# Scaling x by its norm once, before the split, instead of scaling the projections on POOL

## The chip, the cores and the metric

One Trainium2 chip, one core of it. The metric is the device time of one execution in microseconds, as the median of several runs; lower is better. A profile of one execution gives the rows that are quoted below. The engines go by short names: PE is TensorE (matmuls; PEld is its weight load), DVE is VectorE, ACT is ScalarE, POOL is GpSimd, and SP is the engine whose queue issues most DMAs.

## The reference

The kernel computes one layer of a hybrid decoder for 256 tokens of width 1024 in float32, with a final norm:

```python
h = rmsnorm(x, ln_w)                        # x * rsqrt(mean(x*x) + eps) * ln_w
proj = einsum('bsd,de->bse', h, w_in)       # 1024 -> 9216 columns
rq, rk, rv, rg, mq, mk, mv, mg, gr, gm = split(proj)
ret = head_groupnorm(retention(rq, rk, rv)) * silu(rg) @ w_ret_o
mo  = moba_attention(mq, mk, mv) * silu(mg) @ w_moba_o
y   = sigmoid(gr) * ret + sigmoid(gm) * mo
out = rmsnorm(x + y @ w_out, final_norm_w)
```

The norm of x is one number per token. So it can be applied to x ahead of the projection, or to the projection behind it: both give the same product.

## The kernel before, in words

All matrix products run as 24 groups of 512 weight columns, group 0 to group 23. Groups 0 and 1 give the retention's v, groups 2 and 3 its q and k, groups 4 to 9 q, k and v of the other attention (MoBA), groups 10 to 17 the gates, groups 18 to 21 the two branch outputs, groups 22 and 23 the last projection. K is 1024, cut into 8 tiles of 128. The weights of a group come in four chunks of two K tiles (`load`, L77, 512 KB each; the tile `raw` has 6 buffers).

Every operand is split into a high and a low part of 12-bit significands, so that three fast products replace one slow one. For weights that is `split` (L95): ACT copies to `wh` (L108), DVE subtracts to get `wl` (L109); both have 8 buffers, which is two groups. For x it is `split_x` (L149): ACT writes `xh`, DVE `xl` (L152), both with the norm weight of the feature as a scalar, K tile by K tile as x arrives. The norm of the token is not in them.

A group is either N (tokens on the partitions, `proj_n`, L186, three 512-column products per K tile and token tile at L195 to L197) or T (features on the partitions, `proj_t`, L200, per K tile and feature tile a 512-column product at L210 and a 256-column one at L211; four feature tiles per group). The results lie in 4 PSUM banks (`pm`), one per token tile or feature tile.

The norm is computed from a second copy of x: `x_stats` (L168, one number per token and partition, `rs`) and `x_stats_t` (L177), in which PE turns `rs` into a row over all partitions (L180), DVE copies it to `rsb` (L182) and ACT makes `rsq`, the same with the attention's factor (L183). N results are scaled by `rs` as they leave PSUM, at no instruction of their own. T results leave PSUM in `evac_t` (L365): ACT copies one half (L370), DVE adds the other (L371), and POOL multiplies by `rsb` or `rsq` (L372). For q and k there follows `split_to` (L237): ACT copies the high part (L238), POOL subtracts (L239).

The program is written as units, two per group: unit u = 2 * group + half. Ahead of a unit stand the splits of two chunks of the next group, the loads of the group after that, and attention pieces. Each engine executes its own queue in order. The order within the queues is laid out ahead of time by a planner, which lets an engine take the earliest instruction of the program that its estimates call ready; so products of several feature tiles are interleaved when the operands of one are late. On the chip nothing is reordered any more: an instruction that waits holds up all that stand behind it on its engine.

`ret_scores` (L293) makes the masked scores of a retention head: DVE multiplies (L299), ACT and DVE split (L302, L303), and `ret_pv` (L306) is the product with v (L314 to L316).

Of the kernel before, what the change touches and what calls it, by code (L numbers as in the profile page):

```python
"""Hybrid decoder layer (RMSNorm, retention branch, MoBA branch, gated merge, residual, final RMSNorm)
for 256 tokens of width 1024 on one core.

Layouts: a tensor is "N" with tokens on the partitions and "T" with features on the partitions.
Each projection is either N (activations stationary, weights moving, 512 columns) or T (weights
stationary, activations moving, 256 tokens), so that the consumer finds the layout that it needs.

Products with at least 256 moving columns run in float32r (12-bit significands, one pass each): every
operand a is split exactly into a = ah + al with ah = round12(a), al = a - ah, and ah*bh + ah*bl + al*bh are
accumulated in float32. Attention products with 128 moving columns are plain float32 matmuls.  # L10

With 256 tokens the MoBA branch has a single block of 256, so no query has a past block: the top-k
selection is empty for any input, and each query attends causally to its own block.
"""
# [15 lines left out]
P = 128  # L30
# [18 lines left out]
def hybrid_kernel(ctx: ExitStack, tc, xT, x, w_in, gn_w, w_ret_o, w_moba_o, w_out, fn_w, decay, out):  # L49
# [41 lines left out]
    def cut(g, k):  # L91
        """Column ranges in which K tile k of group g is handled."""
        return (slice(0, S), slice(S, GW)) if (g, k) == (0, 0) else (slice(0, GW),)
# [24 lines left out]
    # K tile 0 of group 0 comes in two column ranges: its banks are started by products of zeros.  # L118
# [18 lines left out]
    # rel[q, k] = k - q for the causal pairs, MASKED for the others; query tile 0 with keys 0..127,  # L137
    # query tile 1 with keys 0..255.
# [6 lines left out]

    xs = ac.tile([P, KT, 2, S], F32R, name="xs", tag="xs")
    xh, xl = xs[:, :, 0], xs[:, :, 1]

    def split_x(k):  # L149
        xk = xt[:, KT + k * S:KT + (k + 1) * S]  # L150
        nc.scalar.activation(xh[:, k], xk, AF.Copy, scale=lnw[:, k:k + 1])
        nc.vector.scalar_tensor_tensor(xl[:, k], xk, lnw[:, k:k + 1], xh[:, k].bitcast(F32),  # L152
                                       op0=ALU.mult, op1=ALU.subtract)

    def rsqrt(y, a, tmp):
        """y = a ** -0.5 (a is kept): square root, exact reciprocal, one Newton step."""
        nc.scalar.activation(tmp, a, AF.Sqrt)
        nc.vector.reciprocal(y, tmp)
        nc.vector.tensor_mul(tmp, y, y)
        nc.vector.tensor_mul(tmp, tmp, a)  # L160
        nc.vector.tensor_scalar(tmp, tmp, -0.5, 1.5, op0=ALU.mult, op1=ALU.add)
        nc.vector.tensor_mul(y, y, tmp)
# [3 lines left out]
    rsq = cst.tile([P, S], F32, name="rsq")  # L166

    def x_stats():  # L168
        """1 / rms per token: per partition for N, along the free axis for T."""
        ss = cst.tile([P, NT], F32, name="ss")  # L170
        tmp = cst.tile([P, NT], F32, name="sst")
        for t in range(NT):
            nc.scalar.activation(reto[:, t], xn[:, t], AF.Square, accum_out=ss[:, t:t + 1])
        nc.vector.tensor_scalar(ss, ss, 1.0 / D, EPS, op0=ALU.mult, op1=ALU.add)
        rsqrt(rs, ss, tmp)

    def x_stats_t():  # L177
        ps = pa.tile([P, 512], F32, name="ps_s", tag="s")
        for t in range(NT):
            nc.tensor.matmul(ps[:, t * P:(t + 1) * P], rs[:, t:t + 1].to_broadcast([P, P]), ident,  # L180
                             start=True, stop=True)
        nc.vector.tensor_copy(rsb, ps[:, :S])  # L182
        nc.scalar.activation(rsq, ps[:, :S], AF.Copy, scale=1.0 / math.sqrt(P))  # L183

# [1 line left out]
    def proj_n(g, ah, al, t, c0=0, n=GW, ps=None):  # L186
        """[128 tokens of tile t, n columns of the group from c0], added to ps if that is given."""
# [4 lines left out]
        for k in range(KT):  # L192
            for cs in cut(g, k) if g == 0 else (slice(0, n),):
                h, l = (w[g, k // 2][:, k % 2, c0 + cs.start:c0 + cs.stop] for w in (wh, wl))
                nc.tensor.matmul(ps[:, cs], ah[:, k, sl], h, start=not begun and k == 0, stop=False)  # L195
                nc.tensor.matmul(ps[:, cs], ah[:, k, sl], l, start=False, stop=False)  # L196
                nc.tensor.matmul(ps[:, cs], al[:, k, sl], h, start=False, stop=k == KT - 1)  # L197
        return ps

    def proj_t(g, a, i):  # L200
        """Feature tile i of the group: [128 features, 2, 256 tokens], the two halves still to be added.

        a(k) holds the high and the low part side by side, so that the high part of the weights meets both
        in one product of 512 columns.
        """
# [9 lines left out]
    qT, kT, V = {}, {}, {}  # L215
    # High and low parts of what the scores take in float32r: of the retention all queries and the first
    # 128 keys, of MoBA the last 128 queries and all keys.
    rqs = ac.tile([P, 4, 2, S], F32R, name="rqs", tag="oT")
    early = ac.tile([P, KT + KT * S], F32R, name="early", tag="big8")[:, KT:]
    rks, mq0s = (early[:, c:c + D].rearrange("p (h a s) -> p h a s", a=2, s=P) for c in (0, D))  # L220
    qs, ks = {"r": rqs, 0: mq0s}, {"r": rks}
# [122 lines left out]
    def ret_transpose(i):  # L344
        """Feature tiles 2i, 2i + 1 of the gated retention output, split."""
# [14 lines left out]
    G = {}  # L360
    mT = []
    yTh = yTl = None
    A = None

    def evac_t(g, i, ps):  # L365
        """Feature tile i of group g: adds the two halves of ps and applies what follows."""
        f = (i + 4) if g in (7, 8, 13, 15, 17, 19, 21) else i

        def scaled(out, w, eng=nc.gpsimd):
            nc.scalar.activation(out, ps[:, 1], AF.Copy)  # L370
            nc.vector.tensor_add(out, ps[:, 0], out)  # L371
            eng.tensor_mul(out, out, w)  # L372
# [4 lines left out]
        if g in (4, 7):  # L377
            q = qT[g // 7][:, i]
            scaled(q, rsq)
            split_to(qs[g // 7][:, i], q[:, P:])  # L380
        elif g in (5, 8):
            k = kT[g // 8][:, i]
            scaled(k, rsb)
            split_to(ks[g // 8][:, i], k)
        elif g in (2, 3):
            a = (qT if g == 2 else kT)["r"][:, i]
            scaled(a, rsb)
            split_to((qs if g == 2 else ks)["r"][:, i], a if g == 2 else a[:, :P])
        elif g in (12, 13):
            z, sg = tmp("z"), wk.tile([P, S], F32, name="sg", tag="sg", bufs=2)  # L390
            scaled(z, rsb)
# [3 lines left out]
        elif g in (14, 15, 16, 17):  # L395
            z = tmp("z")
            scaled(z, rsb)
# [4 lines left out]
        elif g in (18, 19):  # L402
            scaled(A[:, f], G[0, f])
        elif g in (20, 21):
            z = tmp("z")
            scaled(z, G[1, f], nc.vector)
            nc.vector.tensor_add(z, z, A[:, f])
            nc.scalar.activation(yTh[:, f], z, AF.Copy)
            nc.vector.tensor_sub(yTl[:, f], z, yTh[:, f].bitcast(F32))

    def evac_n(g, t, ps):
        r1 = rs[:, t:t + 1]

        def split_v():
            h, l = new_v("vh", F32R), new_v("vl", F32R)
            nc.scalar.activation(h, ps, AF.Copy, scale=r1)
            nc.vector.scalar_tensor_tensor(l, ps, r1, h.bitcast(F32), op0=ALU.mult, op1=ALU.subtract)
            return h, l

        if g in (6, 9):  # L420
            if t == 0:
                V["m", g // 9] = split_v()
            else:
                v1 = new_v("v1")
                nc.scalar.activation(v1, ps, AF.Copy, scale=r1)
                V["m", g // 9] += (v1,)
        elif g in (0, 1):
            V["r", g] = V.get(("r", g), ()) + (split_v(),)
        elif g in (10, 11):
            nc.scalar.activation(rgate[:, t, (g - 10) * GW:(g - 9) * GW], ps, AF.Copy, scale=r1)  # L430
# [9 lines left out]
    def unit(g, i):  # L440
        """Half i of group g: a token tile (N) or two feature tiles (T)."""
        nonlocal A, yTh, yTl, rgate
        if i == 0:
            if g == 10:
                rgate = ac.tile([P, NT, D], F32, name="rgate", tag="rgate")
            if g in (2, 4, 7):
                qT["r" if g == 2 else g // 7] = new_qk("qT")
            if g == 5:
# [11 lines left out]
            if g == 20:  # L460
                yT = ac.tile([P, 2, KT, S], F32R, name="yT", tag="xs")
                yTh, yTl = yT[:, 0], yT[:, 1]
        if groups[g][1] == "N":
            evac_n(g, i, proj_n(g, xh, xl, i, ps=ps0[i] if g == 0 else None))
# [27 lines left out]
    # Unit u = 2 * group + half: the attention pieces come before the projection unit that they are set at.  # L492
# [19 lines left out]
    for g in range(NG - 2):  # L512
        for i in range(2):
# [8 lines left out]
            if u == 2:  # L522
                x_stats_t()
            if u == 38:
                # The last columns of x, split: TensorE adds them to the last product.
# [15 lines left out]
    # Output projection, residual and final norm, one token tile after the other. Of the last columns  # L541
    # only what needs them is left for the end.
    r = ac.tile([P, NT, D], F32, name="r", tag="oT")
    sc = cst.tile([P, NT, 5], F32, name="sc")
    for t in range(NT):
        part, a, s, y, v = (sc[:, t, j:j + 1] for j in range(5))
        pieces = ((0, 512), (512, 1024)) if t == 0 else ((0, 512), (512, 768), (768, 1024))
        for j, (c0, c1) in enumerate(pieces):
# [4 lines left out]
            if c1 - c0 == S and last:  # L553
# [3 lines left out]
                proj_n(22 + c0 // GW, yTh, yTl, t, c0 % GW, c1 - c0, ps)  # L557
                nc.scalar.activation(sq, ps, AF.Square, accum_out=ss)
                nc.vector.tensor_mul(rr, ps, ww)
            else:  # L560
                ps = proj_n(22 + c0 // GW, yTh, yTl, t, c0 % GW, c1 - c0)
# [10 lines left out]
        # One Newton step from s, about sqrt(a): sqrt(a) = (s + a / s) / 2; the 2 is in fnw.  # L572
# [14 lines left out]
def _decay_table(np):  # L587
    """decay[m, h, :]: gamma_h ** (n - m) / sqrt(dk) for key m of tile 0 with queries n of 0..255, then for
    key m of tile 1 with the queries of tile 1; 0 where n < m."""
# [37 lines left out]
```

## Time and profile before

| | |
|---|---|
| median of 3 runs | 305.88 us (305.37 to 306.14) |
| profiled execution, first to last instruction | 303.3 us |
| median less span (what lies around it) | 2.6 us |
| PE busy | 294.0 us (97%) |
| DVE busy | 219.7 us (72%) |
| ACT busy | 186.7 us (62%) |
| POOL busy | 79.0 us (26%) |

The profiled execution has its span of 303.3 us; the times of the runs hold some microseconds around that, so that a change is read as a difference of spans and added to the median. A matmul's row lasts longer than the step to the next matmul, since they overlap: the step from start to start is what counts.

### The profile page before, as it was taken

The page shows a single profiled execution, that of the slowest core. Times are in us where ns is not written, and L with a number is a line of the kernel's source. Part 1 is how long each engine was busy: PE and PEld are TensorE (multiplying, and loading weights), DVE is VectorE, ACT ScalarE, POOL GpSimd, SP SyncE. Part 2 cuts the span into 40 slices and gives each one's busy share as a digit, 9 for nine tenths or more (in the row PEclk, how much of TensorE's full clock was granted, in tenths as well). Part 3 has the DMA queues.
Part 4 walks back from the last instruction along what each step waited for, and adds up shares of the span by engine and source line. Part 5 has one row for each costly group of instructions (what it writes and reads, how often), then busy time and mean ns, then how long its engine had stood idle before and what let it go on. Part 6 is the DMA issues. An engine that isn't in the chain of part 4 may idle for free.

```text
span 303.3 us, 4584 instructions
## 1 busy us (share of the span) xinstructions
PE 294.0 (97%) x1628; PEld 253.9 (84%) x1628; DVE 219.7 (72%) x374; ACT 186.7 (62%) x358; POOL 79.0 (26%) x92
## 2 busy tenths in 40 slices
PE   8999989899999999999999999999999999999992
PEld 5778878799988899888888888888888888888891
DVE  3868676868699694884746799685784788899342
ACT  5786655755748676675966657476575556646231
POOL 3000185564520346300000132432432442300000
PEclk9999999999999999999999999999999999999998
DMA  7999967646384552746166264754835759540021
GB/s 188 361 405 407 319 166 244 212 161 193 91 254 108 189 181 100 195 143 218 36 240 200 79 163 123 216 166 168 261 93 201 253 177 304 169 140 0 0 73 69
DMA packets 28969, 55.11 MB, mean 182 GB/s; under 512 B 1937, under 2 KB 3985, under 8 KB 28945
## 3 DMA queue, kind: packets, MB, share of 16 engines
q1 hardware_dynamic: 28624, 54.54, 55.6%
q8 instruction: 13, 0.21, 0.3%
q10 hardware_dynamic: 288, 0.26, 0.3%
q14 instruction: 12, 0.09, 0.1%
q0 software_dynamic: 32, 0.00, 0.0%
HBM read 53.75 MB, written 1.05 MB: 181 GB/s over the span
## 4 chain that ended last, share of the span: by engine, by line
PE 89%; DVE 3%; POOL 3%; ACT 1%; issue 1%; DVEq 0%; ACTq 0%
PE ps_m L210 34%; PE ps_m L211 18%; PE ps_m L196 10%; PE ps_m L195 10%; PE ps_m L197 10%; DVE wl L109 2%; POOL qT L372 2%; POOL rqs L239 1%; PE ps_s L117 1%; PE ps_t L265 1%; ACT wh L108 1%; PE ps_s L244 1%; PE ps_o L284 1%; PE ps_t L351 1%; PE ps_o L316 1%
## 5 line engine op out<-in xcount | busy, mean ns | idle before, releaser
L210 PE MATMUL ps_m<-xs,wh 128*128 128x512 f32 x384 | 134.7, 393 | 0.0
L109 DVE TENSOR_TENSOR wl<-raw,wh 128x1024 fp32r<-128x1024 f32 x88 | 115.4, 1331 | 17.2 <-ACT wh L108 16.8
L211 PE MATMUL ps_m<-xs,wl 128*128 128x256 f32 x384 | 108.1, 282 | 1.1 <-DVE wl L109 1.1
L108 ACT ACTIVATE wh<-raw 128x1024 fp32r<-128x1024 f32 x88 | 90.1, 1052 | 4.4 <-PE ps_m L197 2.0
L210 PEld LDWEIGHTS ps_m<-xs,wh 128*128 128x128 f32 x384 | 72.1, 188 | 14.6
L211 PEld LDWEIGHTS ps_m<-xs,wl 128*128 128x128 f32 x384 | 72.7, 189 | 1.6 <-DVE wl L109 1.4
L372 POOL TENSOR_TENSOR z<-z,rsb 128x256 f32<-128x256 f32 x24 | 23.8, 990 | 88.4 <-DVE z L371 88.4
L196 PE MATMUL ps_m<-wl,xs 128*128 128x512 f32 (+1 forms) x98 | 38.9, 398 | 0.0
L197 PE MATMUL ps_m<-wh,xs 128*128 128x512 f32 (+1 forms) x98 | 38.8, 396 | 0.0
L195 PE MATMUL ps_m<-wh,xs 128*128 128x512 f32 (+1 forms) x98 | 38.7, 403 | 0.0
L196 PEld LDWEIGHTS ps_m<-wl,xs 128*128 128x128 f32 x98 | 19.0, 193 | 4.9 <-DVE wl L106 1.1
L195 PEld LDWEIGHTS ps_m<-wh,xs 128*128 128x128 f32 x98 | 18.9, 194 | 4.4 <-ACT wh L105 0.7
L197 PEld LDWEIGHTS ps_m<-wh,xs 128*128 128x128 f32 x98 | 18.9, 193 | 3.9
L210 PE MATMUL ps_m<-rT,wh 128*128 128x512 f32 x64 | 22.2, 390 | 0.0
L210 PE MATMUL ps_m<-mT,wh 128*128 128x512 f32 x64 | 22.2, 390 | 0.0
L371 DVE TENSOR_TENSOR z<-ps_m,z 128x256 f32<-128x256 f32 x32 | 13.4, 418 | 7.5 <-ACT z L370 7.5
L211 PE MATMUL ps_m<-rT,wl 128*128 128x256 f32 x64 | 18.1, 282 | 0.0
L211 PE MATMUL ps_m<-mT,wl 128*128 128x256 f32 x64 | 18.1, 282 | 0.0
L401 ACT ACTIVATE gt<-z 128x256 f32<-128x256 f32 x16 | 6.7, 418 | 16.8 <-POOL z L372 16.8
L210 PEld LDWEIGHTS ps_m<-rT,wh 128*128 128x128 f32 x64 | 12.0, 188 | 2.5
L210 PEld LDWEIGHTS ps_m<-mT,wh 128*128 128x128 f32 x64 | 12.0, 188 | 2.5
L195 PE MATMUL ps_m<-wh,yT 128*128 128x512 f32 (+1 forms) x40 | 14.0, 350 | 0.0
(171 smaller groups left out, 424.7 us busy)
## 6 DMA issues: line engine op xcount, KB each, us to landing
raw<-in_w_in SPq DMA_DIRECT2D x68, 512.0 KB, 4.7
raw<-in_w_ret_o SPq DMA_DIRECT2D x8, 512.0 KB, 5.1
raw<-in_w_moba_o SPq DMA_DIRECT2D x8, 512.0 KB, 5.0
raw<-in_w_out SPq DMA_DIRECT2D x8, 512.0 KB, 5.7
raw<-in_w_in SPq DMA_DIRECT2D x7, 256.0 KB, 4.5
xn<-in_x SPq DMA_DIRECT2D x2, 512.0 KB, 8.1
xt<-in_xT SPq DMA_DIRECT2D x7, 128.0 KB, 4.5
dec<-in_decay SPq DMA_DIRECT2D x1, 768.0 KB, 10.7
```

Of the source, the lines that this page charges most:

```text
L108: nc.scalar.activation(h, r, AF.Copy)
L109: nc.vector.tensor_sub(l, r, h.bitcast(F32))
L117: nc.tensor.matmul(pw, warm[:, :P], warm, start=True, stop=True)
L195: nc.tensor.matmul(ps[:, cs], ah[:, k, sl], h, start=not begun and k == 0, stop=False)
L196: nc.tensor.matmul(ps[:, cs], ah[:, k, sl], l, start=False, stop=False)
L197: nc.tensor.matmul(ps[:, cs], al[:, k, sl], h, start=False, stop=k == KT - 1)
L210: nc.tensor.matmul(ps, h, a(k), start=k == 0, stop=False)
L211: nc.tensor.matmul(ps[:, 0], l, a(k)[:, 0], start=False, stop=k == KT - 1)
L239: nc.gpsimd.tensor_sub(out[:, 1], a, out[:, 0].bitcast(F32))
L371: nc.vector.tensor_add(out, ps[:, 0], out)
L372: eng.tensor_mul(out, out, w)
L401: nc.scalar.activation(G[g // 16, f], z, AF.Sigmoid)
```

## The change

`x` is split twice. The first split, without the norm of the token, is as before, but goes to two tiles of its own (`x0`) and serves groups 0 and 1 alone. Ahead of units 2 and 3 a new function `norm_x` multiplies x by `rsb` and splits it again, K tile by K tile, into `xs`, which all groups from 2 to 17 use. The multiplication by `rsb` or `rsq` on POOL is gone from groups 2 to 17 (`rsq` too; its factor is now a constant of the ACT and DVE instructions), and N groups from 6 on are no longer scaled by `rs`. The tiles `rqs` and `early`, which share memory with `x0` and with x as loaded, are taken at unit 4. At the end `yT` holds high and low part side by side, as `xs` does.

```diff
+    x0 = [ac.tile([P, KT // 2, 2, S], F32R, name="x0", tag=tag) for tag in ("rgate", "oT")]
     xs = ac.tile([P, KT, 2, S], F32R, name="xs", tag="xs")
+    def x0s(k):
+        return x0[k // 4][:, k % 4]
     def split_x(k):
...
+    def norm_x(k):
+        xk, h, l = xt[:, KT + k * S:KT + (k + 1) * S], xs[:, k, 0], xs[:, k, 1]
+        z = wk.tile([P, S], F32, name="z", tag="z", bufs=4)
+        nc.vector.scalar_tensor_tensor(z, xk, lnw[:, k:k + 1], rsb, op0=ALU.mult, op1=ALU.mult)
+        nc.scalar.activation(h, z, AF.Copy)
+        nc.vector.tensor_sub(l, z, h.bitcast(F32))
...
         nc.vector.tensor_copy(rsb, ps[:, :S])
-        nc.scalar.activation(rsq, ps[:, :S], AF.Copy, scale=1.0 / math.sqrt(P))
...
-        def scaled(out, w, eng=nc.gpsimd):
-            nc.scalar.activation(out, ps[:, 1], AF.Copy)
-            nc.vector.tensor_add(out, ps[:, 0], out)
-            eng.tensor_mul(out, out, w)
+        def halves(out, w=1.0):
+            nc.scalar.activation(out, ps[:, 1], AF.Copy, scale=w)
+            if w == 1.0:
+                nc.vector.tensor_add(out, ps[:, 0], out)
+            else:
+                nc.vector.scalar_tensor_tensor(out, ps[:, 0], w, out, op0=ALU.mult, op1=ALU.add)
...
-            scaled(q, rsq)
+            halves(q, 1.0 / math.sqrt(P))
...
-            scaled(k, rsb)
+            halves(k)
...
         elif g in (18, 19):
-            scaled(A[:, f], G[0, f])
+            halves(A[:, f])
+            nc.gpsimd.tensor_mul(A[:, f], A[:, f], G[0, f])
...
             if u == 2:
                 x_stats_t()
+            if u in (2, 3):
+                for k in range(4 * (u - 2), 4 * (u - 1)):
+                    norm_x(k)
```

## Rows read from the trace of the kernel before

**Rows 1.** The page, part 1: busy time of each engine, share, instructions.

```profile
PE 294.0 (97%) x1628; PEld 253.9 (84%) x1628; DVE 219.7 (72%) x374; ACT 186.7 (62%) x358; POOL 79.0 (26%) x92
```

**Rows 2.** Busy time in four stretches; the header names the columns.

```profile
core 0: us, PE busy (x) PEld busy (x) DVE busy (x) ACT busy (x) POOL busy (x), PEclk, DMA share, GB/s
29.00:62.00 33.00, 30.79 (x181) 27.03 (x180) 23.45 (x26) 20.10 (x34) 17.43 (x17) 1.00 0.77 244
62.00:297.40 235.40, 235.40 (x1335) 206.20 (x1334) 175.09 (x307) 144.93 (x288) 59.11 (x65) 1.00 0.50 156
297.40:303.30 5.90, 0.00 (x0) 0.00 (x0) 1.70 (x7) 1.28 (x4) 0.00 (x0) 0.76 0.24 89
```

**Rows 3.** Timeline of PE, 24 to 62 us: start, duration, instruction, [idle <-releaser].

```profile
26.22 0.61 PE L180 MATMUL ps_s<-ident,rs 128*128 128x128 f32 x4
...
28.99 0.40 PE L210 MATMUL ps_m<-xs,wh 128*128 128x512 f32 x1
29.22 0.28 PE L211 MATMUL ps_m<-xs,wl 128*128 128x256 f32 x1
29.34 0.40 PE L210 MATMUL ps_m<-xs,wh 128*128 128x512 f32 x1
...
42.20 0.39 PE L210 MATMUL ps_m<-xs,wh 128*128 128x512 f32 x1
43.69 0.39 PE L211 MATMUL ps_m<-xs,wl 128*128 128x256 f32 x1 [1.10 <-DVE wl L109]
...
58.92 0.28 PE L315 MATMUL ps_o<-vl,ih 128*128 128x256 f32 x1
60.30 0.39 PE L316 MATMUL ps_o<-vh,il 128*128 128x256 f32 x1 [1.11 <-DVE il L303]
```

**Rows 4.** Timeline of DVE, 26 to 44 us.

```profile
26.11 1.22 DVE L109 TENSOR_TENSOR wl<-raw,wh 128x1024 fp32r<-128x1024 f32 x1
27.24 0.75 DVE L417 SCALAR_TENSOR_TENSOR vl<-ps_m,rs,vh 128x512 fp32r<-128x512 f32 x1
27.90 0.42 DVE L182 COPY rsb<-ps_s 128x256 f32<-128x256 f32 x1
28.23 0.74 DVE L417 SCALAR_TENSOR_TENSOR vl<-ps_m,rs,vh 128x512 fp32r<-128x512 f32 x1
29.91 0.75 DVE L417 SCALAR_TENSOR_TENSOR vl<-ps_m,rs,vh 128x512 fp32r<-128x512 f32 x1 [0.93 <-ACT vh L416]
31.13 3.50 DVE L109 TENSOR_TENSOR wl<-raw,wh 128x1024 fp32r<-128x1024 f32 x3 [0.47 <-ACT wh L108]
35.98 0.42 DVE L371 TENSOR_TENSOR qT<-ps_m,qT 128x256 f32<-128x256 f32 x1 [1.36 <-ACT qT L370]
...
42.03 1.61 DVE L109 TENSOR_TENSOR wl<-raw,wh 128x1024 fp32r<-128x1024 f32 x1 [1.70 <-ACT wh L108]
```

**Rows 5.** Timelines of POOL, ACT and DVE around the two waits of PE.

```profile
38.88 1.72 POOL L372 TENSOR_TENSOR qT<-qT,rsb 128x256 f32<-128x256 f32 x1
40.63 0.42 ACT L238 ACTIVATE rqs<-qT 128x256 fp32r<-128x256 f32 x1 [1.73 <-POOL qT L372]
58.20 1.63 POOL L372 TENSOR_TENSOR kT<-kT,rsb 128x256 f32<-128x256 f32 x1 [2.03 <-DVE kT L371]
59.17 1.08 DVE L303 TENSOR_TENSOR il<-inn,ih 128x384 fp32r<-128x384 f32 x1
```

**Rows 6.** Groups of instructions by form: out<-in, count, then busy us, mean ns, idle before.

```profile
L372 POOL TENSOR_TENSOR z<-z,rsb 128x256 f32<-128x256 f32 x24 | 23.8, 990 | 88.4 <-DVE z L371 88.4
L152 DVE SCALAR_TENSOR_TENSOR xs<-xt,xs 128x256 fp32r<-128x256 f32 x8 | 3.8, 481 | 3.9 <-ACT xs L151 3.9
L409 DVE TENSOR_TENSOR yT<-z,yT 128x256 fp32r<-128x256 f32 x8 | 3.4, 424 | 1.5 <-ACT yT L408 1.5
L408 ACT ACTIVATE yT<-z 128x256 fp32r<-128x256 f32 x8 | 3.3, 413 | 9.0 <-DVE z L407 9.0
L303 DVE TENSOR_TENSOR il<-inn,ih 128x384 fp32r<-128x384 f32 x4 | 2.9, 725 | 1.8 <-ACT ih L302 1.7
```

More of the change, by code (lines that the diff above doesn't have):

```diff
@@ L144, in hybrid_kernel @@
                                 compare_op=ALU.is_ge, fill=MASKED, base=base, channel_multiplier=1)
+    x0 = [ac.tile([P, KT // 2, 2, S], F32R, name="x0", tag=tag) for tag in ("rgate", "oT")]
     xs = ac.tile([P, KT, 2, S], F32R, name="xs", tag="xs")
-    xh, xl = xs[:, :, 0], xs[:, :, 1]
+    def x0s(k):
+        return x0[k // 4][:, k % 4]
     def split_x(k):
[L150 to L153, printed above, removed]
+        xk, (h, l) = xt[:, KT + k * S:KT + (k + 1) * S], (x0s(k)[:, j] for j in range(2))
+        nc.scalar.activation(h, xk, AF.Copy, scale=lnw[:, k:k + 1])
+        nc.vector.scalar_tensor_tensor(l, xk, lnw[:, k:k + 1], h.bitcast(F32), op0=ALU.mult, op1=ALU.subtract)
+    def norm_x(k):
[4 more added lines that the diff above has]
+        nc.vector.tensor_sub(l, z, h.bitcast(F32))
     def rsqrt(y, a, tmp):
@@ L165, in hybrid_kernel @@
     rsb = cst.tile([P, S], F32, name="rsb")
-    rsq = cst.tile([P, S], F32, name="rsq")
     def x_stats():
@@ L182, in x_stats_t, with proj_n @@
         nc.vector.tensor_copy(rsb, ps[:, :S])
-        nc.scalar.activation(rsq, ps[:, :S], AF.Copy, scale=1.0 / math.sqrt(P))
-    def proj_n(g, ah, al, t, c0=0, n=GW, ps=None):
+    def proj_n(g, a, t, c0=0, n=GW, ps=None):
         begun = ps is not None
@@ L194, in proj_n @@
                 h, l = (w[g, k // 2][:, k % 2, c0 + cs.start:c0 + cs.stop] for w in (wh, wl))
-                nc.tensor.matmul(ps[:, cs], ah[:, k, sl], h, start=not begun and k == 0, stop=False)
-                nc.tensor.matmul(ps[:, cs], ah[:, k, sl], l, start=False, stop=False)
-                nc.tensor.matmul(ps[:, cs], al[:, k, sl], h, start=False, stop=k == KT - 1)
+                nc.tensor.matmul(ps[:, cs], a(k)[:, 0, sl], h, start=not begun and k == 0, stop=False)
+                nc.tensor.matmul(ps[:, cs], a(k)[:, 0, sl], l, start=False, stop=False)
+                nc.tensor.matmul(ps[:, cs], a(k)[:, 1, sl], h, start=False, stop=k == KT - 1)
         return ps
@@ L215, in hybrid_kernel @@
     qT, kT, V = {}, {}, {}
[L218 to L221, printed above, removed]
+    qs, ks = {}, {}
     oT = None
@@ L361, in hybrid_kernel @@
     mT = []
-    yTh = yTl = None
+    yT = None
     A = None
@@ L386, in evac_t @@
             a = (qT if g == 2 else kT)["r"][:, i]
-            scaled(a, rsb)
+            halves(a)
             split_to((qs if g == 2 else ks)["r"][:, i], a if g == 2 else a[:, :P])
@@ L390, in evac_t @@
             z, sg = tmp("z"), wk.tile([P, S], F32, name="sg", tag="sg", bufs=2)
-            scaled(z, rsb)
+            halves(z)
             nc.scalar.activation(sg, z, AF.Sigmoid)
@@ L396, in evac_t @@
             z = tmp("z")
-            scaled(z, rsb)
+            halves(z)
             if i % 2 == 0:
@@ L402, in evac_t, with split_v @@
         elif g in (18, 19):
-            scaled(A[:, f], G[0, f])
+            halves(A[:, f])
+            nc.gpsimd.tensor_mul(A[:, f], A[:, f], G[0, f])
         elif g in (20, 21):
             z = tmp("z")
-            scaled(z, G[1, f], nc.vector)
+            halves(z)
+            nc.vector.tensor_mul(z, z, G[1, f])
             nc.vector.tensor_add(z, z, A[:, f])
-            nc.scalar.activation(yTh[:, f], z, AF.Copy)
-            nc.vector.tensor_sub(yTl[:, f], z, yTh[:, f].bitcast(F32))
+            nc.scalar.activation(yT[:, f, 0], z, AF.Copy)
+            nc.vector.tensor_sub(yT[:, f, 1], z, yT[:, f, 0].bitcast(F32))
     def evac_n(g, t, ps):
-        r1 = rs[:, t:t + 1]
-        def split_v():
+        def split_v(r1=1.0):
             h, l = new_v("vh", F32R), new_v("vl", F32R)
             nc.scalar.activation(h, ps, AF.Copy, scale=r1)
-            nc.vector.scalar_tensor_tensor(l, ps, r1, h.bitcast(F32), op0=ALU.mult, op1=ALU.subtract)
+            if g < 2:
+                nc.vector.scalar_tensor_tensor(l, ps, r1, h.bitcast(F32), op0=ALU.mult, op1=ALU.subtract)
+            else:
+                nc.vector.tensor_sub(l, ps, h.bitcast(F32))
             return h, l
@@ L424, in evac_n @@
                 v1 = new_v("v1")
-                nc.scalar.activation(v1, ps, AF.Copy, scale=r1)
+                nc.scalar.activation(v1, ps, AF.Copy)
                 V["m", g // 9] += (v1,)
         elif g in (0, 1):
-            V["r", g] = V.get(("r", g), ()) + (split_v(),)
+            V["r", g] = V.get(("r", g), ()) + (split_v(rs[:, t:t + 1]),)
         elif g in (10, 11):
-            nc.scalar.activation(rgate[:, t, (g - 10) * GW:(g - 9) * GW], ps, AF.Copy, scale=r1)
+            nc.scalar.activation(rgate[:, t, (g - 10) * GW:(g - 9) * GW], ps, AF.Copy)
     def ret_silu(t, c):
@@ L440, in unit @@
     def unit(g, i):
-        nonlocal A, yTh, yTl, rgate
+        nonlocal A, yT, rgate
         if i == 0:
@@ L447, in unit @@
                 qT["r" if g == 2 else g // 7] = new_qk("qT")
+            if g == 2:
+                qs["r"] = ac.tile([P, 4, 2, S], F32R, name="rqs", tag="oT")
+                early = ac.tile([P, KT + KT * S], F32R, name="early", tag="big8")[:, KT:]
+                ks["r"], qs[0] = (early[:, c:c + D].rearrange("p (h a s) -> p h a s", a=2, s=P) for c in (0, D))
             if g == 5:
@@ L460, in unit @@
             if g == 20:
-                yT = ac.tile([P, 2, KT, S], F32R, name="yT", tag="xs")
-                yTh, yTl = yT[:, 0], yT[:, 1]
+                yT = ac.tile([P, KT, 2, S], F32R, name="yT", tag="xs")
         if groups[g][1] == "N":
-            evac_n(g, i, proj_n(g, xh, xl, i, ps=ps0[i] if g == 0 else None))
+            evac_n(g, i, proj_n(g, x0s if g < 2 else lambda k: xs[:, k], i, ps=ps0[i] if g == 0 else None))
         else:
@@ L539, in hybrid_kernel, with ya @@
         split(NG - 1, c)
+    def ya(k):
+        return yT[:, k]
     r = ac.tile([P, NT, D], F32, name="r", tag="oT")
@@ L556, in hybrid_kernel @@
                 nc.tensor.matmul(ps, ir, xr[:, S:], start=False, stop=False)
-                proj_n(22 + c0 // GW, yTh, yTl, t, c0 % GW, c1 - c0, ps)
+                proj_n(22 + c0 // GW, ya, t, c0 % GW, c1 - c0, ps)
                 nc.scalar.activation(sq, ps, AF.Square, accum_out=ss)
@@ L560, in hybrid_kernel @@
             else:
-                ps = proj_n(22 + c0 // GW, yTh, yTl, t, c0 % GW, c1 - c0)
+                ps = proj_n(22 + c0 // GW, ya, t, c0 % GW, c1 - c0)
                 nc.vector.tensor_add(rr, ps, xn[:, t, c0:c1])
```

## The prediction

> **What bounds the kernel now.** I read the busy times first, then the stretches, then the timelines of the engines where PE waits. PE is busy for 294.0 of 303.3 us [rows 1]. The stretches say where the other 9.3 us lie: between 62 and 297.4 us PE has no idle time at all, 235.40 of 235.40 us, and behind its last product stand 5.9 us of tail that end the final norm [rows 2]. Neither is touched by the change. What PE loses in the middle are two single waits. At 42.20 it stands 1.49 us until the next start, where the usual step behind such a product is 0.23 (28.99 to 29.22), so it loses 1.27 us to a low part of weights that DVE delivers late; at 58.92 the step is 1.38 us where 0.12 is usual (29.22 to 29.34), so it loses 1.26 us to the low part of the first retention head's scores [rows 3]. The rest of the idle time is the start, before x has come. So all that a faster path through POOL can give back is 1.27 + 1.26 = 2.5 us, whatever happens in the other 235 us.
>
> POOL is where both waits begin. ACT stands 1.73 us at 40.63 for a multiplication on POOL that took 1.72 us, and the split of the weights behind it in ACT's queue is late by that; so DVE starts the low part only at 42.03, idle for 1.70 us before [rows 4, 5]. At 59.17 DVE's subtraction for the scores takes 1.08 us beside a multiplication on POOL that runs until 59.83; the four of them have a mean of 0.725, so the other three take (4 x 0.725 - 1.08) / 3 = 0.61 us [rows 5, 6].
>
> **What goes.** 48 multiplications leave POOL: the row shows 24 of them at a mean of 0.99 us, and the q and k of six groups have the other 24 [rows 6]. Some 45 us of POOL's 79 go, nearly all of it at 62 us or later beside a PE that never waits, so it is worth nothing there. Between 29 and 62 us it removes ACT's stops, and with them the cause of both waits: up to 2.5 us, bounded below by nothing. I take both as gone, for two reasons: DVE's idle 1.70 us at 42.03 is ACT's stop alone, and at 59.17 the 0.47 us of slower subtraction go, with more coming from ACT's earlier splits. `rsq` goes (one short ACT instruction). The scale constants ride on instructions that are there anyway; adding the factor to DVE's addition of a half I cost at nothing to 0.06 us each (0.48 against 0.42 for the two kinds of two-input instruction [rows 6]), hidden under PE. The other order of `yT`, the two `x0` tiles and the later taking of `rqs` and `early` add no instruction; `rqs` and `early` must wait for group 1 and for `norm_x`, but the first results that go there are those of group 2, whose products come behind both.
>
> **What comes.** Eight times a DVE multiplication (like L152, 0.48 us), an ACT copy (like L408, 0.41) and a DVE subtraction (like L409, 0.42) [rows 6]. Queued back to back DVE's instructions overlap: 26.11 to 27.24 is 1.13 us for one of 1.22, 27.90 to 28.23 is 0.33 for one of 0.42 [rows 4]. So I take 0.09 off: 0.39 + 0.33 = 0.72 us of DVE per K tile, 5.8 us for all eight, and some 2.6 us of ACT.
>
> The place is what matters. They can't begin before `rsb`, which DVE has copied at 28.23, 0.8 us before PE's first product of group 2 at 28.99; and that product needs the new `xs`. Before, `xs` was ready from the start. DVE's own queue had free time here (0.93, 0.47 and 1.36 us before 35.98 [rows 4]), but not 5.8 us of it.
>
> I carry the queues forward by hand from 28.23, each engine taking the earliest ready instruction of the program, with the steps of the rows. First K tile: 28.23 + 0.39 (multiply) + 0.41 (ACT) + 0.42 (subtract) and hand-overs gives 29.6 to 29.9, so PE starts group 2 0.6 to 0.9 us late. DVE then owes until the last K tile: eight K tiles at 0.72 (5.8 us), two splits of weights at 1.13 (2.3 us), two low parts of v at 0.66 (27.24 to 27.90; 1.3 us), together 9.4 us: the last K tile is there at 37.6. PE meanwhile needs per K tile and feature tile one step of 0.35 us (28.99 to 29.34 [rows 3]), 32 steps for the group, 11.15 us. Of the four banks the fourth comes free only behind the second low part of v, which stands behind `norm_x` in the program; so PE can work on K tiles 0 to 3 of three feature tiles, 12 steps or 4.2 us, to about 34.1. The fifth K tile comes at 35.3 to 36.3, behind both splits and four more multiplications: a second wait of 1.2 to 2.2 us, with up to 0.3 between. From then on K tiles come at 0.72 us against 1.05 for three steps, and PE waits no more. Sum of the new waits: 1.8 to 3.4 us; I take 2.7. The ends: 0.6 us, if everything behind the first K tile hides, and 9.4 us less nothing, if PE's queue held only products that need the last K tile.
>
> Does it run on? DVE owes group 3 four splits and four additions, 4 x 1.13 + 4 x 0.33 = 5.9 us, to 43.5; PE ends group 2 at 28.99 + 11.15 + 2.7 = 42.8 and needs the last chunk six steps later, at 44.9. So the shift is not handed on, and the old wait at 42.20 has no successor. ACT and SP: the loads hang on DVE's low parts, up to 4 us later for the group 4 chunks, and those are wanted behind 53 us; covered.
>
> Sum: + 2.7 - 1.27 - 1.26 = + 0.2 us. The planner's queues never quite fit the chip (at 42.20 PE waits though DVE had idled for 4.5 us in the four gaps of [rows 4]), and a new dense place has more to misfit; I add 0.2. Span 303.3 + 0.4 = 303.7; the median stands 2.6 us above the span, so 306.3 us. Between runs 0.3% (0.9 us) can't be told from no change.
>
> **A rule weighed.** PE's granted clock stays at 1.00 over the two old waits and is 0.76 in the tail, where PE has nothing to do [rows 2]. The Trainium skill (TensorE: Matmul & The Clock Gate, "Part 1: The HAM clock gate") says that an idle TensorE falls from 2.4 to 1.2 GHz and must earn the higher clock again; the trace agrees for the tail. It speaks against the change, as the waits at group 2 are longer together than any one before; it is the third rival.
>
> **Rivals.** First, faster: the planner fills the gaps better than my hand does (the second low part of v ahead of `norm_x` frees the fourth bank, worth 4 steps or 1.4 us; K tile 4 ahead of a split). For it: 2.8 us of DVE's idle time before 35.98, and PE's interleaving at 29 to 42 without a wait. Against it: the program puts `norm_x` first. Then the new waits are 0.6 to 1.4, the old ones gone: - 1.1 to - 1.9, say 304.4 us.
>
> Second, slower: PE's queue is laid out on estimates in which the K tiles come sooner than they do, and a product that waits in order holds up those that could run. Place: group 2, 29 to 38 us. It decides as soon as PE has fewer than some ten steps to do before the fifth K tile: with two feature tiles open instead of three it is 4 steps, 1.4 us more, and if PE then stands until the last K tile at 37.6 with two tiles begun, it has done 8 steps of 32 and ends 24 x 0.35 = 8.4 us later, at 46.0, 5.9 us late; less 2.5 this is + 3.4. Or one of the old waits stays, + 1.3. So + 1.2 to + 3.4, say 307.8 us. For it: the same queues gave the wait at 42.20. Against it: between 29 and 42 the order fitted.
>
> Third, the clock: a wait of 3 us at a stretch, and the products behind it at the lower level. A 512-column step of 0.23 us would take twice that; over some 3 us of products behind the wait it costs about 1.5 us on top of a long wait: + 1.9, 308.2 us or more. Against it: the waits come in two or three pieces, and 1.27 us did nothing to the clock.
>
> **Numbers.** Forecast 0.42, faster rival 0.25, slower rival 0.28, clock 0.05. The forecast's own range is 305.3 to 307.2: 0.36 of it within 0.9 us of before, 0.06 above. Of the faster rival 0.23 lies below 304.98, of the slower 0.24 above 306.8. Faster 0.23, same 0.42, slower 0.35. The range that should hold it is 304.0 to 308.9: the faster rival's best end below, and above it the slower one but for its last part.
>
> **What would show it.** In the profile after: the first L210 starts at 29.6 to 29.9 and waits for DVE; a second wait before 37 us; PE without a wait from there to its last product; POOL's busy time near 34 us; DVE without idle time from 24 to 38 us. A wait at 42 to 62 us, or waits before 40 us that sum to less than 1.5 or more than 3.5 us, would make it wrong.

## The result, and the profile after

The changed kernel takes 307.75 us (307.58 to 307.93, 4 runs) against 305.81 us before: 1.94 us slower by the medians, ratio 1.0065 with an interval of 1.0051 to 1.008. The forecast was 306.3 us and "no change" as the likeliest case; the time lies inside the range and near the second rival's 307.8 us. One run of the kernel below that loads x earlier took 593.69 us, for which nothing here gives a reason, and its ratio leaves that run out.

The busy times of the page come first. POOL's work has halved, DVE's is the same, and PE has no less to do ([rows 1] before):

```profile
PE 293.8 (96%) x1628; PEld 252.8 (83%) x1628; DVE 219.4 (72%) x390; ACT 192.3 (63%) x365; POOL 37.9 (12%) x44
```

The stretches answer to [rows 2]; columns are PE, PEld, DVE, ACT and POOL busy, granted clock, DMA share, GB/s.

```profile
29.00:62.00 33.00, 29.07 (x166) 25.20 (x165) 28.84 (x44) 22.86 (x41) 11.35 (x8) 1.00 0.73 245
62.00:299.80 237.80, 237.75 (x1353) 208.46 (x1352) 170.08 (x308) 147.96 (x288) 24.00 (x25) 1.00 0.49 155
299.80:305.70 5.90, 0.00 (x0) 0.00 (x0) 1.69 (x7) 1.28 (x4) 0.00 (x0) 0.93 0.24 89
```

From 62 us on PE works without a gap, as before, and the tail is 5.90 us, as before. The loss lies between 29 and 62 us, where PE is busy for 29.07 us instead of 30.79. Its timeline there, against [rows 3]:

```profile
29.49 0.40 PE L207 MATMUL ps_m<-wh,x 128*128 128x512 f32 x1
32.47 0.47 PE L220 MATMUL ps_m<-xs,wh 128*128 128x512 f32 x1 [2.58 <-DVE xs L164]
...
35.55 0.28 PE L221 MATMUL ps_m<-xs,wl 128*128 128x256 f32 x1
37.17 0.50 PE L220 MATMUL ps_m<-xs,wh 128*128 128x512 f32 x1 [1.35 <-DVE xs L164]
```

The step from 29.49 to 32.47 is 2.98 us where 0.23 is usual: 2.74 us lost. The one from 35.55 to 37.17 is 1.62 us where 0.12 is usual: 1.51 us lost (both from unrounded times). Together 4.25 us of new waits, both for `xs`, the product of `norm_x`. The two old waits (1.27 and 1.26 us) are gone: + 4.25 - 2.53 = + 1.7 us, near the 1.94 of the medians. The two profiled spans differ by 2.4 us; the other 0.7 is that group 2 would have started at 29.72 here and at 28.99 before, by waits for the first weights. They differ from profile to profile, with the change and without it: of the first 20 us PE is busy for 18.83 before and 17.97 here, for 18.82 in the changed kernel with the copies on DVE below, and for 18.32 in the kernel before without POOL's multiplications.

Why the first wait is so long is read from two timelines side by side. First DVE, which answers to [rows 4]:

```profile
28.64 0.42 DVE L193 COPY rsb<-ps_s 128x256 f32<-128x256 f32 x1
28.97 0.74 DVE L427 SCALAR_TENSOR_TENSOR vl<-ps_m,rs,vh 128x512 fp32r<-128x512 f32 x1
29.63 1.66 DVE L162 SCALAR_TENSOR_TENSOR z<-xt,rsb 128x256 f32<-128x256 f32 x4
31.89 1.43 DVE L164 TENSOR_TENSOR xs<-z,xs 128x256 fp32r<-128x256 f32 x4 [0.60 <-ACT xs L163]
33.24 2.36 DVE L109 TENSOR_TENSOR wl<-raw,wh 128x1024 fp32r<-128x1024 f32 x2
35.51 1.27 DVE L162 SCALAR_TENSOR_TENSOR z<-xt,rsb 128x256 f32<-128x256 f32 x3
36.70 0.76 DVE L164 TENSOR_TENSOR xs<-z,xs 128x256 fp32r<-128x256 f32 x2
...
37.77 0.75 DVE L427 SCALAR_TENSOR_TENSOR vl<-ps_m,rs,vh 128x512 fp32r<-128x512 f32 x1
```

Then ACT, which makes the copies between DVE's multiplications (L162) and subtractions (L164):

```profile
29.92 0.69 ACT L425 ACTIVATE vh<-ps_m,rs 128x512 fp32r<-128x512 f32 x1 [1.99 <-PE ps_m L207]
30.51 1.05 ACT L108 ACTIVATE wh<-raw 128x1024 fp32r<-128x1024 f32 x1
31.46 1.32 ACT L163 ACTIVATE xs<-z 128x256 fp32r<-128x256 f32 x4
```

The first multiplication (0.48 us) is done at 30.1, but its copy starts at 31.46. ACT is held by two instructions ahead of it in its queue: one that waits for the last product of group 1, and a split of weights. Meanwhile DVE runs all four multiplications in a row, then idles 0.60 us. In PE's second wait the fifth K tile is late for the cause that the prediction names: two splits (33.24 to 35.6) and three more multiplications stand ahead of it. How long the wait is depends also on how much work PE had until then, which is taken up further down.

### The profile page after: what moved, and what is told of

Same layout as the page of the kernel before. It is cut to its first block, busy times and chain, and to the rows that moved or that the text cites. A ratio compares the mean times of both kernels' runs of the same rounds, so it can differ in the third digit from the quotient of the medians.

```text
span 305.7 us, 4545 instructions
## 1 busy us (share of the span) xinstructions
PE 293.8 (96%) x1628; PEld 252.8 (83%) x1628; DVE 219.4 (72%) x390; ACT 192.3 (63%) x365; POOL 37.9 (12%) x44
## 3 DMA queue, kind: packets, MB, share of 16 engines
HBM read 53.75 MB, written 1.05 MB: 179 GB/s over the span
## 4 chain that ended last, share of the span: by engine, by line
PE 90%; DMA 4%; DVE 3%; SPq 1%; ACT 1%; issue 0%; DVEq 0%; ACTq 0%
PE ps_m L220 37%; PE ps_m L221 20%; PE ps_m L206 9%; PE ps_m L207 9%; PE ps_m L205 8%; DMA raw<-in_w_in 2%; DMA xt<-in_xT 2%; DVE wl L109 1%; PE ps_t L272 1%; SPq L87 1%; ACT wh L108 1%; PE ps_s L251 1%; PE ps_o L291 1%; PE ps_t L358 1%; DVE xs L164 1%; SPq L85 1%
## 5 line engine op out<-in xcount | busy, mean ns | idle before, releaser
L109 DVE TENSOR_TENSOR wl<-raw,wh 128x1024 fp32r<-128x1024 f32 x88 | 110.1, 1273 | 14.0 <-ACT wh L108 13.6
L205 PE MATMUL ps_m<-wh,xs 128*128 128x512 f32 x64 | 25.5, 399 | 0.0
L207 PE MATMUL ps_m<-wh,xs 128*128 128x512 f32 x64 | 25.3, 396 | 0.0
L206 PE MATMUL ps_m<-wl,xs 128*128 128x512 f32 x64 | 25.3, 396 | 0.0
L413 POOL TENSOR_TENSOR A<-A,gt 128x256 f32<-128x256 f32 x8 | 6.8, 854 | 120.1 <-DVE A L379 120.1
L377 ACT ACTIVATE z<-ps_m 128x256 f32<-128x256 f32 x32 | 12.1, 379 | 13.2 <-PE ps_m L221 13.0
L207 PEld LDWEIGHTS ps_m<-wh,xs 128*128 128x128 f32 x64 | 12.0, 188 | 2.9
L206 PEld LDWEIGHTS ps_m<-wl,xs 128*128 128x128 f32 x64 | 12.0, 188 | 2.5
L205 PEld LDWEIGHTS ps_m<-wh,xs 128*128 128x128 f32 x64 | 12.0, 188 | 2.5
```

Source lines behind the costliest of these rows:

```text
L109: nc.vector.tensor_sub(l, r, h.bitcast(F32))
L205: nc.tensor.matmul(ps[:, cs], a(k)[:, 0, sl], h, start=not begun and k == 0, stop=False)
L206: nc.tensor.matmul(ps[:, cs], a(k)[:, 0, sl], l, start=False, stop=False)
L207: nc.tensor.matmul(ps[:, cs], a(k)[:, 1, sl], h, start=False, stop=k == KT - 1)
L377: nc.scalar.activation(out, ps[:, 1], AF.Copy, scale=w)
L413: nc.gpsimd.tensor_mul(A[:, f], A[:, f], G[0, f])
```

## The experiments

Three things were to be told apart: whether the old waits really begin with POOL, what makes `norm_x` dear (the order of ACT's queue, the late arrival of `rsb`, or too little room on DVE), and whether the gain can be had without the price. "Before" below is the kernel before, run beside each on the same chip; every ratio is against it. The queues are laid out anew for each kernel.

**POOL's multiplications left out of the kernel before.**

```diff
-            eng.tensor_mul(out, out, w)
+            if w is not None:
+                eng.tensor_mul(out, out, w)
...
-            scaled(q, rsq)
+            scaled(q, None)
```

(so for all of groups 2 to 17)

> The kernel before with the multiplications by the norm on POOL left out of groups 2 to 17 and nothing put in their place: x is not normed for the T groups (that part of the computation is left out). Theory: both old waits of PE (1.27 us at 42.2 and 1.26 us at 58.9) begin with POOL, so both go and nothing else changes: 2.5 us less, 303.3 us, PE without a wait from 20 to 297 us. Rival: the waits are DVE's own load and stay, 305.8 us; half gone would be 304.5 us.

Measured: 302.99 us, ratio 0.9919 (0.9895 to 0.9942). The waits of PE, all of them (for whom, total us, times, longest):

```profile
PE ps_s L117 <- DVE warm L114: 1.2, 1, 1.2
PE ps_m L195 <- ACT wh L105: 0.5, 1, 0.5
```

Both are of the start, the second one for the first weights. So the old waits are POOL's, and removing its work is worth some 2.5 us (the waits) to 2.9 us (the medians). By the medians the change stands 4.8 us above this kernel: that is what `norm_x` costs before the gain on POOL is taken off.

**POOL's multiplications put back into the changed kernel.**

```diff
             halves(k)
+            nc.gpsimd.tensor_mul(k, k, one)
```

(so for all of groups 2 to 17)

> The changed kernel with the multiplications on POOL put back, by a tile of ones, so that norm_x and POOL's work are both there. Theory: the new waits of 2.74 and 1.51 us at group 2 are norm_x's alone and stay; POOL's two waits come back in part or in whole behind them, 308 to 310.3 us. Rival: POOL's waits are absorbed by the delay of PE, 307.8 us as the changed kernel.

Measured: 308.92 us, ratio 1.0107 (1.0092 to 1.0122). PE's waits:

```profile
PE ps_m L222 <- DVE xs L164: 2.6, 1, 2.6
PE ps_s L117 <- DVE warm L114: 1.2, 1, 1.2
PE ps_o L325 <- DVE il L312: 1.1, 1, 1.1
PE ps_o L323 <- ACT ih L311: 0.3, 1, 0.3
```

The old second wait is back at 1.1 us, on the same tile `il`; the old first one (weights of group 3) isn't, absorbed by the delay of group 2. So the prediction's two steps are there one by one: removal ends the waits, `norm_x` makes others. The second of the new waits is missing, for a reason that the timeline and the stretches of this kernel show:

```profile
29.12 0.40 PE L209 MATMUL ps_m<-wh,x 128*128 128x512 f32 x1
32.09 0.47 PE L222 MATMUL ps_m<-xs,wh 128*128 128x512 f32 x1 [2.58 <-DVE xs L164]
...
33.10 0.40 PE L223 MATMUL ps_m<-xs,wl 128*128 128x256 f32 x1
...
33.95 0.63 PE L222 MATMUL ps_m<-xs,wh 128*128 128x512 f32 x1
34.37 0.41 PE L223 MATMUL ps_m<-xs,wl 128*128 128x256 f32 x1
34.59 0.63 PE L222 MATMUL ps_m<-xs,wh 128*128 128x512 f32 x1
```

```profile
32.00:33.00 1.00, 0.91 (x5) 0.85 (x6) 1.00 (x4) 1.00 (x3) 0.00 (x0) 1.00 0.70 268
33.00:36.00 3.00, 3.00 (x12) 2.56 (x11) 3.00 (x5) 2.60 (x4) 0.00 (x0) 0.52 0.33 84
```

After the same wait of 2.74 us the granted clock is 0.52 from 33 to 36 us, the lower of the two levels (1.2 GHz), and a pair of products takes 0.64 us (33.95 to 34.59) instead of 0.35. PE then spends, working slowly, the time in which the changed kernel waits for the fifth K tile.

**The copies by DVE.**

```diff
-        nc.scalar.activation(h, z, AF.Copy)
+        nc.vector.tensor_copy(h, z)
```

> The changed kernel with the high part of norm_x copied by DVE in place of ACT. Theory 1 (ACT's queue order: the copies stand behind the evacuation of group 1 that waits for PE, and behind a split of weights): PE's first wait falls from 2.74 to about 1.3 us, since DVE now makes a K tile by itself, and the second grows by the copies' 2 to 3 us of DVE less what ACT's order had cost; 306 to 308 us. Theory 2 (DVE has too little room, order is nothing): DVE gets 2.6 us more to do, so the waits together grow by as much: 310 us.

Measured: 307.12 us (305.31 to 308.99, 10 runs), ratio 1.0043 (1.0018 to 1.0068). The interval meets that of the change, so the time alone doesn't decide. The profile is of the run of 305.31 us, the shortest of the ten; on the mechanism it shows three waits for `xs` that sum to 2.5 us, the longest 1.1, in place of 2.58 and 1.35. More work for DVE, and less waiting: room on DVE is not what made the first wait. The second wait didn't grow, though theory 1 had it so. The ten runs spread over 3.7 us, and the four longest (307.43 to 308.99) are those with a mean clock of 0.99 to 0.991; what that does is seen better in the next kernel.

```profile
PE ps_m L220 <- DVE xs L164: 2.5, 3, 1.1
```

**ACT's order alone.**

```diff
+        high[k] = nc.scalar.activation(h, z, AF.Copy)
...
-                split(g + 1, c)
+                with tc.issue_after(high[3].ins) if u == 3 else nullcontext(): split(g + 1, c)
...
-            unit(g, i)
+            with tc.issue_after(high[3].ins) if u == 3 else nullcontext(): unit(g, i)
```

> The changed kernel with one order forced: ACT queues the splits of unit 3 and the evacuation of group 1's second token tile behind the first four copies of norm_x. No instruction is added or taken away. Theory 1 (order): PE's first wait falls from 2.74 to 1.2 to 1.6 us; the second stays or grows by less: 306.2 to 307.2 us. Theory 2 (room): the last K tile comes as late as before, the second wait takes what the first gives, 307.75 us.

Measured: 306.72 us (306.25 to 308.61, 9 runs), ratio 1.0042 (1.0022 to 1.0062). ACT's copies now come first, and PE's first wait shrinks:

```profile
30.66 1.21 ACT L163 ACTIVATE xs<-z 128x256 fp32r<-128x256 f32 x3 [2.20 <-DVE z L162]
32.85 0.42 ACT L163 ACTIVATE xs<-z 128x256 fp32r<-128x256 f32 x1 [0.99 <-DVE z L162]
```

```profile
30.05 0.40 PE L207 MATMUL ps_m<-wh,x 128*128 128x512 f32 x1
31.90 0.48 PE L220 MATMUL ps_m<-xs,wh 128*128 128x512 f32 x1 [1.45 <-DVE xs L164]
```

31.90 - 30.05 - 0.23 = 1.62 us instead of 2.74, with not one instruction more or less. The second wait is 0.97 us (32.91 to 34.00, less 0.12):

```profile
32.91 0.28 PE L221 MATMUL ps_m<-xs,wl 128*128 128x256 f32 x1
34.00 0.80 PE L220 MATMUL ps_m<-xs,wh 128*128 128x512 f32 x1 [0.81 <-DVE xs L164]
...
37.26 0.39 PE L220 MATMUL ps_m<-xs,wh 128*128 128x512 f32 x1
```

```profile
33.00:36.00 3.00, 2.19 (x8) 1.72 (x7) 3.00 (x6) 3.00 (x7) 0.00 (x0) 0.62 0.18 66
36.00:37.00 1.00, 1.00 (x5) 0.90 (x4) 1.00 (x3) 1.00 (x3) 0.00 (x0) 0.50 0.38 70
```

The two waits sum to 2.6 us instead of 4.25, yet the profiled run took 308.17 us. Behind its second wait the granted clock is at the lower level (0.62 on average from 33 to 36 us, 0.50 from 36 to 37): the five steps from 34.00 to 37.26 take 3.26 us where 5 x 0.35 = 1.75 is usual, 1.5 us lost. The nine runs fall into two groups that fit this price: six with a mean clock of 0.994 to 0.996 took 306.25 to 306.73 us, three with 0.99 took 307.89 to 308.61. The median is one of the six. It moved as the theory of order says, by 1.0 us; the interval still touches that of the change.

**The wait for the statistics taken away.**

```diff
-        nc.vector.scalar_tensor_tensor(z, xk, lnw[:, k:k + 1], rsb, op0=ALU.mult, op1=ALU.mult)
+        nc.vector.scalar_tensor_tensor(z, xk, lnw[:, k:k + 1], one, op0=ALU.mult, op1=ALU.mult)
```

> The changed kernel with norm_x multiplying by a tile of ones that is there from the start, in place of rsb: the norm of the token is left out for groups 2 to 17, the work of norm_x is the same. It takes away only that norm_x must wait for the statistics. Theory 1 (lateness: rsb comes 0.3 us before group 2's start): norm_x moves into the gaps of DVE and ACT before 29 us, PE's waits at group 2 fall from 4.25 us to under 1.5, 303.0 to 304.8 us. Theory 2 (room: DVE is full from 17.7 to 29 us, 9.33 of 11.3 us busy, and norm_x wants 5.8 us): the waits move to groups 1 and 2 but stay near 3 to 4 us, 306.5 to 307.8 us.

Measured: 303.98 us, ratio 0.9949 (0.9933 to 0.9965). PE's waits:

```profile
PE ps_s L117 <- DVE warm L114: 1.2, 1, 1.2
PE ps_m L208 <- DVE wl L109: 0.9, 1, 0.9
PE ps_m L207 <- ACT wh L105: 0.4, 1, 0.4
```

With the same work of `norm_x`, none of the waits at group 2 is left. What remains is 0.9 us at group 1, for weights that DVE now delivers later (0.3 in the changed kernel). So lateness explains most: 307.75 less 303.98 is 3.8 us, of the 4.8 that `norm_x` costs. Room explains about 1 at most; this kernel's interval meets that of the one without POOL's multiplications (0.9895 to 0.9942). The 1.0 us of ACT's order isn't to be added to the 3.8: `norm_x` done early has its copies elsewhere in ACT's queue too.

**x loaded earlier.**

```diff
     for c in range(4):
+        if c < 2:
+            nc.sync.dma_start(xn[:, c], xr[:, c])
         load(1, c)
-        if c % 2:
-            nc.sync.dma_start(xn[:, c // 2], xr[:, c // 2])
```

> The changed kernel with the second copy of x loaded earlier: each half goes ahead of one chunk of group 1's weights (in place of behind two and four). Theory 1 (lateness): the statistics and rsb come some 3 us earlier, and PE's waits at group 2 fall from 4.25 to under 2 us; group 1's weights come 1.3 to 2.6 us later, which costs PE 0.5 to 2 us: 305.3 to 307 us. Theory 2 (room): DVE is as full as before, 307.5 to 308.5 us.

Measured: 305.54 us, ratio 1.0004 (0.999 to 1.0018). Here the result is the full computation, and lateness is cut in part: `rsb` is copied at 26.08 instead of 28.64, and PE waits for `xs` once, 0.7 us.

```profile
26.08 0.42 DVE L193 COPY rsb<-ps_s 128x256 f32<-128x256 f32 x1
```

```profile
PE ps_m L220 <- DVE xs L164: 0.7, 1, 0.7
PE ps_m L206 <- DVE wl L109: 0.5, 1, 0.5
```

The change and this kernel have intervals that don't touch (1.0051 to 1.008, and 0.999 to 1.0018): the order of two loads is worth the whole loss against the kernel before. It doesn't give the gain: this kernel stands 2.6 us above the one without POOL's multiplications.

**`norm_x` two groups later, in two places.** Groups 2 and 3 then take `x0` and are scaled by DVE. Since `x0` is needed longer, half of it, `early` and the scratch of the statistics are also placed or taken otherwise; the cut shows the main lines, for units 5 and 6.

```diff
+            nc.vector.tensor_mul(a, a, rsb)
...
-            if u in (2, 3):
-                for k in range(4 * (u - 2), 4 * (u - 1)):
+            if u in (5, 6):
+                for k in range(4 * (u - 5), 4 * (u - 4)):
```

> The changed kernel with norm_x moved from units 2 and 3 to units 5 and 6: groups 0 to 3 use x0, groups 2 and 3 are scaled by eight multiplications on DVE, groups 4 to 17 use the normed x as in the change. Same norm_x work. Theory: norm_x costs time only since group 2 must wait for it; with two groups between, PE waits for nothing, 303.2 to 304.2 us. Rival: DVE has no room in groups 2 and 3 either (5.8 for norm_x and 3.4 us for the multiplications, against 4.5 to 6 idle from 29 to 52 us), and PE waits 2 to 4 us for weights: 305.5 to 307.5 us.

> The kernel of e7_norm_later with norm_x one unit earlier, at units 4 and 5 in place of 5 and 6. Theory: e7's wait of 2.2 us at the first retention scores comes from norm_x standing ahead of the split of the first k tiles, both in DVE's queue and through the memory that `early` shares with x as loaded; one unit earlier it is out of the way and nothing waits: 303 to 304.5 us. Rival: norm_x in group 2 delays the low parts of group 3's weights, and PE waits 1 to 3 us at 40 to 45 us: 304.5 to 307 us.

Measured: 307.53 us, ratio 1.0069 (1.005 to 1.0088), for units 5 and 6; 305.71 us, ratio 1.0006 (0.999 to 1.0021), for units 4 and 5. Both theories missed. The times lie at or in the rivals' ranges, but PE doesn't wait for weights behind 20 us in either, so the rivals' mechanism isn't there. The waits at group 2's start are gone in both, as the theory said, but PE waits elsewhere; first the row of units 5 and 6:

```profile
PE ps_s L243 <- POOL early L247: 2.0, 1, 2.0
```

then those of units 4 and 5:

```profile
PE ps_m L221 <- DVE qT L383: 0.8, 1, 0.8
PE ps_s L243 <- POOL early L247: 0.6, 1, 0.6
```

The first retention scores wait for the split of k (`early`), which comes behind `norm_x`; one unit earlier this falls from 2.0 to 0.6 us, and PE waits 0.8 us for DVE to empty a bank instead. How much of it is DVE's queue, and how much the memory that `early` shares with x as loaded, wasn't separated. And a wait of 2.0 us is less than half of the 4.5 us by which units 5 and 6 stand above the kernel without POOL's multiplications; the rest stays open.

**Only what causes the old waits, moved.** The kernel before with the eight multiplications of groups 2 and 3 on DVE:

```diff
         elif g in (2, 3):
-            scaled(a, rsb)
+            scaled(a, rsb, nc.vector)
```

> The kernel before with one thing changed: the eight multiplications by the norm in groups 2 and 3 run on DVE in place of POOL. x is split once, as before. Theory: both old waits begin with POOL's multiplications in these two groups; DVE has 4.5 us idle there and the eight take 3.4, so both go: 303.2 to 303.8 us, PE without a wait from 20 to 297 us. Rival: DVE's own queue then delivers the low parts as late as POOL's stops did, or the multiplications of groups 4 and 5 on POOL take over: 304.5 to 306 us.

Measured: 302.52 us (302.21 to 303.06), ratio 0.9905 (0.989 to 0.992). PE's stretches:

```profile
20.00:62.00 42.00, 42.00 (x238) 36.73 (x238) 35.38 (x54) 27.96 (x50) 13.06 (x12) 1.00 0.87 300
62.00:294.50 232.50, 232.50 (x1319) 203.48 (x1317) 172.53 (x301) 143.50 (x284) 58.05 (x61) 1.00 0.48 154
```

PE is busy for all of 274.5 us. POOL keeps 40 of the 48 multiplications, and that costs nothing. This beats both kernels, with one argument changed. The gain of 3.3 us is larger than the two waits (2.53) and than the theory's range; where the other 0.8 comes from isn't shown.

## Why the prediction was right and wrong

- **Right: what bounds the kernel.** PE has no wait from 62 us on before and after, so 35 us less of POOL there (59.11 to 24.00) are worth nothing; the gain is the two waits, 2.53 us. With POOL's work left out the kernel gains 2.9 us, and one wait comes back when the work does.
- **Wrong: the start of group 2.** "First K tile: 28.23 + 0.39 (multiply) + 0.41 (ACT) + 0.42 (subtract)" gave a first wait of 0.6 to 0.9 us; it was 2.74. The step took DVE and ACT as free for it. DVE had the low part of a v tile in between (28.97 to 29.63, 0.66 us; it stands right behind `rsb` in [rows 4] too, and the text counts it only toward the last K tile), and ACT's queue held an evacuation that waits for group 1's last product, and a split, ahead of the copy: from 30.1 to 31.46 the first K tile did not move, 1.4 us. 0.66 and 1.4 on top of some 0.7 make the 2.74. The forced order gives back 1.1 of it (2.74 to 1.62).
- **Right in size, in part by luck: the second wait**, forecast as 1.2 to 2.2 us at 34.1 and measured as 1.51 us at 35.55. That it is for the fifth K tile, behind two splits and more multiplications, is as the text says. But the text gives PE twelve steps on the first four K tiles, and PE had nine: 18 products from 32.47 to 35.67, the row of 32.50 to 35.60 below. Three banks were free, as the text has it: DVE's low parts of v have emptied them by 29.7, and the one for the fourth comes at 37.77. With twelve steps PE would have worked until 36.7, and the wait would have been some 0.5 us; that is a count, no run shows it. A start that is 2 us later than forecast and three steps too few nearly cancel.
- **Right: nothing behind it.** PE has no wait from 37.2 us to the last product, and the old wait at 42.20 has no successor.
- **So the sum**: forecast 1.8 to 3.4 us, taken at 2.7; measured 4.25, outside the bound for which the text said it would be wrong (3.5). The sum failed by its first term, and the 0.2 us that the text adds for queues that never quite fit didn't cover it. The time is near that of the second rival, a queue of PE laid out on estimates (0.28, 307.8 us), but the rival's mechanism has only a part in it: the three steps that PE's queue didn't have ready, 3 x 0.35 = 1.05 us by the count above. The kernel with ACT's order forced shows that order of PE once more, as PE waits at 34.00 for the fourth K tile after three steps, though three K tiles and three free banks allow nine. The larger part, the 2 us at the first K tile, comes from the queues of DVE and ACT, which the rival doesn't name.
- **The third rival**, the clock, is real, and what it costs depends on what PE would have done at that time. The profiled run of the change keeps 1.00 from 32.5 to 35.6 us, as the row below shows, while the kernel with POOL put back falls to 0.52 after an equal wait. The change's other three runs show a mean of 0.988 to 0.99 against 0.999, and the spans are 305.4 to 305.7 us in both. That fits a fall in the time in which PE would next have waited for DVE, as in the kernel with POOL put back; no profile of these three runs shows it. Where ACT's order is forced, the same fall costs 1.5 us, which is the price that the rival gave it. The Trainium skill (TensorE: Matmul & The Clock Gate, "Part 1: The HAM clock gate") has the fall to half the clock after idling; the 0.52 agrees. Why one of two equal waits is followed by it and the other isn't, no run here shows.

```profile
32.50:35.60 3.10, 3.10 (x18) 2.69 (x18) 3.10 (x6) 3.10 (x4) 0.00 (x0) 1.00 0.35 119
```

- **The signs** that the text named: no wait at 42 to 62 us, as forecast, but the first product of group 2 starts at 32.47 (forecast 29.6 to 29.9), DVE idles 0.60 us ahead of its subtractions at 31.89 (forecast none), and POOL is busy for 37.9 us (forecast near 34), as its subtractions for q got slower (last section).
- **Not weighed: when `rsb` comes.** The text took 28.23 as given. That moment decided most of the outcome: the kernel that doesn't wait for it is 0.5% faster than before, and the one that loads x a few transfers earlier is as fast as before within its interval.

## What to carry to other kernels

Work that is moved ahead of a busy engine's next product must be priced with the queue of every engine in its chain, at the moment when it arrives: here 0.41 us of copying waited 1.4 us behind two instructions that had nothing to do with it. When a helper engine causes a wait, look for the few instructions that do so before removing all of them: 8 of 48 multiplications made both waits, and moving those eight gave 1%, where removing all at the price of new work ahead of PE lost 0.65%. And where new work hangs on a late input, try the input's load order first: here it gave back the loss, though not the gain.

## What the runs showed that was not expected

After equal waits of 2.74 us the granted clock fell in one kernel's profile (0.52 for some 3 us) and stayed at 1.00 in another's; the fall came while PE was at work again, about 1 us behind the wait (its products lengthen from 33.10 on, the wait ends at 32.09). In the kernel with ACT's order forced two shorter waits, 1.62 and 0.97 us with 1.1 us of products between them, were followed by it.

POOL's subtractions for the retention's q have POOL to themselves now and take longer: a mean of 1.87 us in the changed kernel, where the same four had 0.95 before, beside a DVE that has no pause there.

```profile
L246 POOL TENSOR_TENSOR rqs<-qT,rqs 128x256 fp32r<-128x256 f32 x4 | 7.4, 1870 | 39.5 <-ACT rqs L245 39.5
```
